# The modulation blocks that fill TensorE's gaps are issued in pairs instead of singly

## The chip, the cores and the metric

The kernel runs on one core of one Trainium2 chip. The metric is the device time of one execution in microseconds; three runs of the kernel before gave 1457.76, 1460.0 and 1465.21, so the time to beat is their median, 1460.0 us. A core has five instruction streams that run side by side and meet at semaphores: TensorE (PE, with its weight loads PEld), VectorE (DVE), ScalarE (ACT), GpSimd (POOL) and SyncE (SP), which here issues most of the transfers.

## The reference

Two layers of a hybrid block over 512 latent and 256 context tokens of width 1024. Each layer first turns the conditioning vector into six vectors per stream (adaLN), then does a mixer with three head groups (attention, a Mamba-2 scan called SSD, a Hyena long convolution) and a mixture of 16 experts:

```python
def adaln(cvec, w_mod, b_mod):                    # w_mod[i]: (1024, 6*1024)
    m = jax.nn.silu(cvec) @ w_mod + b_mod
    return jnp.split(m, 6, axis=-1)

for i in range(DEPTH):                            # DEPTH = 2
    sh1, sc1, gt1, sh2, sc2, gt2 = adaln(c, w_mod[i], b_mod[i])          # latent
    csh1, csc1, cgt1, csh2, csc2, cgt2 = adaln(c_ctx[None], w_mod[i], b_mod[i])
    hl = modulate(rmsnorm(xl, g_mix[i]), sh1, sc1)
    q_l, k_l, v_l, z_l, xbc_l, dt_l, hy_l = split_proj(hl @ w_in[i])
    ...   # attention over 768 keys; bidirectional SSD in chunks of 128; Hyena by FFT
    mix_l = jnp.concatenate([att_l, ssd_l, hyn_l], axis=-1) @ w_out[i]
    xl = xl + gt1[:, None, :] * mix_l
    hl2 = modulate(rmsnorm(xl, g_ffn[i]), sh2, sc2)
    xl = xl + gt2[:, None, :] * grouped_moe(hl2, ...)                     # top 2 of 16
    ...   # layer 0 does the same for the context tokens
return rmsnorm(xl, g_final)
```

The modulation matrix is large (6144 columns per layer, two layers) and is read for only two vectors (`c` and `c_ctx`), so its cost is mostly the transfer of its weights. Only the first two of layer 0's six vectors are needed before the first projection; all others are needed later.

## The kernel before

The 96 column blocks of the two modulation matrices (48 per layer, 128 columns each) are computed by `adaln` (L243). One block is two transfers of 256 KB into tiles called `mraw` (L254, issued on SP) and eight narrow f32 matmuls (L256), four per tile, which the trace shows as sixteen records. Four blocks share one PSUM bank (`AG = 4`); after the fourth, DVE copies the bank to `ms` (L260), and when the group after it has started its second block, `adaln_end` (L232) multiplies `ms` by a selector on PE (L238) and adds the bias on DVE (L239, tile `mcol`). The pool `md` has `MB = 4` buffers of `mraw`, which is two blocks. SP issues in order: a transfer whose buffer is still being read holds all transfers behind it.

Sixteen blocks are computed inside `norm1`, before the projections of layer 0. The other 80 are "filler": the iterator `fill` lists them, and `filler(n)` takes the next n. It is called inside the projections of layer 0 (`proj_feat`, L445, at steps k = 0, 3 and 6 of each weight block), by the generator `fillers` that is woven between the SSD, the attention heads and the attention, and in `convolutions` (two per step, `HF_ = 2`). `filler(96)` takes whatever is left before layer 0's output projection. In layer 1 the list is empty.

The order of instructions is not the written one. `weave` alternates generators by fixed ratios, and on top of that the framework reorders each engine's stream with a simulated timeline: an instruction that is ready in that timeline may be moved ahead of one that is not. So filler matmuls stand where the simulated PE would otherwise wait, and a small shift in the timeline of layer 0 can change which ready instruction comes first much later, in layer 1, where no line was edited.

Layer 1's mixer matters for the prediction. Three generators are woven after the projections: `ssd` (L720) with `attention` (L913) and `hy_conv` (L516). `ssd` goes over four chunks of 128 tokens. Each chunk needs a tile `G` of 768 KB (L731, a broadcast read issued on SP), then masks on POOL (L735), twelve exponentials on ACT (L738), a sum on POOL (L740), two products on DVE (L745), and matmuls on PE (L767 with `G`, L769 with the chunk's entering state `H`). In layer 1 `G` has one buffer (`GB = (2, 1)`), so the read for the next chunk waits until PE has read the last. `hy_conv` reads its filter tiles `Kt` (L528), also one buffer, in the same SP queue.

Of the kernel before, what the change touches and what calls it, by code (L numbers as in the profile page):

```python
# [3 lines left out]

# [136 lines left out]
def tile_kernel(tc, I, out, dbg=None):  # L141
# [89 lines left out]
    late, part = [], {}  # L231
# [10 lines left out]
    def adaln(l, ch, wp, mb, j, n, step, wp2=None):  # L242

        if j == AD:
            adaln_end()
        if j == 0:
            part["ps"] = bank("d")
        ps = part["ps"]
        for h in range(2):
            if h and wp2:  # L250
                raw = wp2.tile([P, 4, P], F32, name="mraw", tag="mraw", bufs=MB)
            else:
                raw = wp.tile([P, 4, P], F32, name="mraw", tag="mraw", bufs=mb)
            SP.dma_start(raw, I["wm"][l, :, ch, h])  # L254
            for k in range(4):
                PE.matmul(ps[32 * k:32 * k + 32, 0:P], c32[:, 4 * h + k, 30 - 2 * j:62 - 2 * j], raw[:, k],  # L256
                          start=(j + h == 0), stop=(j == n - 1 and h == 1))
        if j == n - 1:
            ms = wp.tile([P, P], F32, name="ms", bufs=2)
            DVE.tensor_copy(ms, ps[:, 0:P])  # L260
            late.append((l, slice(ch - j * step, ch + 1, step), n, ms))
# [197 lines left out]
    def proj_feat(wp, l, off, hh, hl, use, filler=None, kind="b"):  # L459
        wh, wl = wload(wp, l, off, 1024)  # L460
        for c, t0, n in ((0, 0, NLAT), (1, NLAT, NCTX)):
            if not use[c]:
                continue
            ps = bank(kind)
            for k in range(8):
                if filler and c == 0 and k in FK:
                    filler(1)
                s = slice(k * P, (k + 1) * P)
                mm3(ps[:, 0:n], wh[:, s], wl[:, s], hh[:, k, t0:t0 + n], hl[:, k, t0:t0 + n], k == 0, k == 7)
            yield c, ps[:, 0:n], n  # L470
# [7 lines left out]
    def to_tokens(src, n, cb, par, ps):  # L478
        for jt in range(n):
            PE.transpose(ps[:, jt * P:(jt + 1) * P], src[:, par + jt * 256:par + jt * 256 + 255:2], ident)  # L480

    def hy_proj(l, wp, hh, hl, pool, u, filler):

        use = (True, l == 0)
# [4 lines left out]
        for b in range(6):  # L489
            cb = b % 2  # L490
            for c, ps, m in proj_feat(wp, l, WI_HY + b * 1024, hh, hl, use, filler):
                zh, zl, x1, x2 = u[c]
                n = m // 256
                cw, cv = lv(l, VL_HW + 3 * b, 3), lv(l, VL_HB + b)
                if b >= 4:
                    conv(x2[:, cb], ps, m, cw, cv)
                    if c == len(u) - 1:
                        yield
                    continue
                d = wp.tile([P, 512], F32, name="ud", tag="ud", bufs=UB[l])  # L500
                conv(d[:, 0:m], ps, m, cw, cv)
                pt = bank("b")
                for par in range(2):
                    to_tokens(d, n, cb, par, pt[:, par * n * P:(par + 1) * n * P])
                src = pt[:, 0:2 * n * P].rearrange("p (a j w) -> p a j w", a=2, j=n)
                cs = slice(cb * P, (cb + 1) * P)
                if b < 2:
                    for par in range(2):
                        ACT.copy(zh[:, par, :, cs], src[:, par])
                        DVE.tensor_sub(zl[:, par, :, cs], src[:, par], f(zh[:, par, :, cs]))  # L510
                else:
                    for par in range(2):
                        ACT.copy(x1[:, par, :, cs], src[:, par])
                if c == len(u) - 1:
                    yield
# [1030 lines left out]
    for l in range(DEPTH):  # L1546
# [54 lines left out]
        fill = iter([(0, c) for c in range(16, 48)] + [(1, c) for c in range(48)] if l == 0 else [])  # L1601
# [6 lines left out]
            yield  # L1608

        def filler(n):  # L1610
            for _ in range(n):
                for m, c0 in fill:
                    adaln(m, c0, md, MB, c0 % AG, AG, 1)
                    break

        def fillers():
            while True:
# [136 lines left out]
        with tc.issue_after(mark.ins):  # L1754
# [5 lines left out]
            for n in (2, 4):  # L1760
                m, h = D // n, P // n
# [203 lines left out]
```

## Time and profile before

| what | value |
|---|---|
| three runs, median | 1457.76, 1460.0, 1465.21; 1460.0 us |
| the profiled execution | 1466.34 us, of which span 1464.4 us |
| PE matmul busy | 1248.4 us, 85% of the span |
| PE weight loads busy | 899.8 us, 61% |
| DVE, ACT, POOL busy | 760.8 (52%), 488.4 (33%), 453.9 (31%) us |
| mean granted TensorE clock | 0.925 |
| modulation matmuls (L256) | 1536 records, 72.8 us of PE |

PE is the busiest engine by far and its idle time is spread over all stages. A busy share is an average: what a shift in one stage is worth is read from that stage. The granted clock is shown as a share of full speed: 1.00 is 2.4 GHz and 0.50 is 1.2 GHz. Line numbers are those of the kernel before; one line is added at the top and two in `filler`, so a line below both has a number larger by three in the `order` rows of the changed kernel (by one for lines above `filler`).

### The profile page before, as it was taken

How to read it: one execution, taken by the hardware profiler on the slowest of the kernel's cores; microseconds unless marked ns; L12 is line 12 of the kernel's file. 1: busy time of each engine (PE TensorE's matmuls, PEld its weight loads, DVE VectorE, ACT ScalarE, POOL GpSimd, SP SyncE). 2: the span in 40 equal slices, each digit the busy share in tenths (PEclk: the TensorE clock that was granted, in tenths of full speed). 3: DMA queues.
4: the chain of work that ended last, by engine and by line, in shares of the span. 5: the costliest groups of instructions: out<-in, count | busy, mean ns of one | idle time of the engine just before them, and what ended most of it. 6: DMA issues, size and time to landing. Idle time of an engine off the chain costs nothing. (4 is left out here: it accounts for less than half of the span.)

```text
span 1464.4 us, 23682 instructions
## 1 busy us (share of the span) xinstructions
PE 1248.4 (85%) x8904; PEld 899.8 (61%) x8904; DVE 760.8 (52%) x1661; ACT 488.4 (33%) x1056; POOL 453.9 (31%) x497
## 2 busy tenths in 40 slices
PE   5999999899899899869998949988988888599780
PEld 2787787677677677634544428876776776345440
DVE  6854652644667875852332334754498475512121
ACT  4332334445233453311110144444454542111111
POOL 3220321544334524222323311321188412222221
PEclk9999999997799999979998969999999899699995
DMA  7744536343655163279999551111301173999954
GB/s 295 241 157 158 173 102 215 118 152 132 206 161 184 58 244 117 86 275 369 340 322 279 110 173 44 58 58 44 138 30 58 41 288 129 352 371 353 354 115 137
DMA packets 88809, 265.04 MB, mean 181 GB/s; under 512 B 10397, under 2 KB 13101, under 8 KB 88048
## 3 DMA queue, kind: packets, MB, share of 16 engines
q1 hardware_dynamic: 76016, 224.39, 43.5%
q0 software_dynamic: 12672, 39.07, 10.4%
q8 instruction: 72, 1.18, 0.3%
q14 instruction: 49, 0.40, 0.1%
HBM read 231.62 MB, written 31.79 MB: 180 GB/s over the span
## 5 line engine op out<-in xcount | busy, mean ns | idle before, releaser
L1417 PE MATMUL bank<-we,xh 128*32 128x128 f32 (+3 forms) x1280 | 208.7, 394 | 12.1 <-DVE y L1473 8.6
L1417 PEld LDWEIGHTS bank<-we,xh 128*32 128x32 f32 (+3 forms) x1280 | 99.5, 139 | 106.1 <-issue 76.9
L219 PE MATMUL bank<-hh,hw 128*128 128x512 f32 (+1 forms) x440 | 159.5, 362 | 0.1
L220 PE MATMUL bank<-hl,hw 128*128 128x512 f32 (+1 forms) x440 | 157.1, 357 | 0.0
L221 PE MATMUL bank<-hh,lw 128*128 128x512 f32 (+1 forms) x440 | 156.7, 356 | 0.4 <-DVE lw L207 0.4
L1474 POOL DMA_INDIRECT xd<-y,txi x35 | 56.6, 1618 | 177.7 <-DMA xd<-y,txi 90.2
L1417 PE MATMUL bank<-we,gh 128*32 128x256 f32 (+3 forms) x392 | 101.0, 522 | 2.8 <-ACT gh L1450 1.4
L219 PEld LDWEIGHTS bank<-hh,hw 128*128 128x128 f32 x440 | 85.4, 194 | 12.1 <-issue 1.0
L221 PEld LDWEIGHTS bank<-hh,lw 128*128 128x128 f32 x440 | 84.6, 192 | 12.8 <-DVE lw L207 0.9
L220 PEld LDWEIGHTS bank<-hl,hw 128*128 128x128 f32 x440 | 85.0, 193 | 11.4 <-issue 0.8
L930 POOL TENSOR_SCALAR pt<-pt,su 128x768 f32<-128x768 f32 (+1 forms) x60 | 55.0, 924 | 118.6 <-DVE su L929 97.6
L256 PE MATMUL bank<-mraw,c 128*32 128x128 f32 x1536 | 72.8, 295 | 16.9 <-DMA mraw<-in_wm_dram 11.8
L1393 POOL DMA_INDIRECT xg<-hd,tk x40 | 40.4, 1009 | 96.6 <-PE bank L1407 32.7
L207 DVE TENSOR_TENSOR lw<-rw,hw 128x1024 fp32r<-128x1024 f32 (+1 forms) x36 | 44.7, 1243 | 49.1 <-ACT hw L206 48.9
L256 PEld LDWEIGHTS bank<-mraw,c 128*32 128x32 f32 x1536 | 41.2, 114 | 41.4 <-DMA mraw<-in_wm_dram 16.0
L945 PE MATMUL bank<-ph,vt 128*64 128x128 f32 x624 | 53.8, 292 | 15.1 <-DVE ph L942 7.0
L1417 PEld LDWEIGHTS bank<-we,gh 128*32 128x32 f32 (+3 forms) x392 | 35.7, 143 | 49.6 <-issue 41.8
L220 PE MATMUL bank<-lo,mh 128*128 128x512 f32 x160 | 63.8, 399 | 1.5 <-DVE lo L207 1.5
L219 PE MATMUL bank<-ho,mh 128*128 128x512 f32 x160 | 64.5, 405 | 0.4 <-ACT ho L206 0.4
L221 PE MATMUL bank<-ho,ml 128*128 128x512 f32 x160 | 63.2, 395 | 0.0
L206 ACT CAST hw<-rw 128x1024 fp32r<-128x1024 f32 (+1 forms) x36 | 37.8, 1049 | 76.1 <-PE bank L220 48.0
L923 DVE TENSOR_REDUCE mx<-banks 128x1 f32<-128x768 f32 (+1 forms) x60 | 50.3, 844 | 23.3 <-PE banks L920 23.1
(478 smaller groups left out, 2744.9 us busy)
## 6 DMA issues: line engine op xcount, KB each, us to landing
we<-in_we_dram SPq DMA_DIRECT2D x192, 512.0 KB, 11.3
mraw<-in_wm_dram SPq DMA_DIRECT2D x192, 256.0 KB, 3.6
rw<-in_wi_dram SPq DMA_DIRECT2D x34, 512.0 KB, 3.5
ro<-in_wo_dram SPq DMA_DIRECT2D x16, 512.0 KB, 4.9
G<-ar SPq DMA_DIRECT2D x10, 768.0 KB, 3.9
xd<-ox SPq DMA_DIRECT2D x10, 512.0 KB, 2.7
hd<-h POOLq DMA_DIRECT2D x10, 512.0 KB, 2.9
xf<-xd SPq DMA_DIRECT2D x10, 512.0 KB, 7.0
```

The costliest lines, as they stand in the source:

```text
L206: ACT.copy(hi, src)
L207: (lo_eng or DVE).tensor_sub(lo, src, f(hi))
L219: PE.matmul(o, lh, rh, start=start, stop=False)
L220: PE.matmul(o, lh, rl, start=False, stop=False)
L221: PE.matmul(o, ll, rh, start=False, stop=stop)
L256: PE.matmul(ps[32 * k:32 * k + 32, 0:P], c32[:, 4 * h + k, 30 - 2 * j:62 - 2 * j], raw[:, k], start=(j + h == 0), stop=(j == n - 1 and h = ...
L923: DVE.tensor_reduce(mx, ps, axis=AX.XY, op=OP.max)
L930: POOL.tensor_scalar(pt[:, 0:nkt * P], pt[:, 0:nkt * P], su, 1.0, OP.mult, OP.mult)
L945: PE.matmul(po[64 * q:64 * q + 64, 0:P], vt[:, k0 + kt + j, h // 3], ph[:, (2 * j + q) * P:(2 * j + q + 1) * P], start=(kt + j == 0), stop ...
L1393: POOL.indirect_dma_start(out=xg[0:c], out_offset=None, in_=hd, in_offset=bass.IndirectOffsetOnAxis(ap=R.token(i)[0:c], axis=0))
L1417: PE.matmul(ps[r:r + c, 0:m], lh[:, 0:c], w[:, m * j:m * j + m], start=start, stop=stop)
L1474: POOL.indirect_dma_start(out=xd.rearrange("t (n m) -> (t n) m", n=n), out_offset=bass.IndirectOffsetOnAxis(ap=R.row(i)[r], axis=0), in_=y ...
```

## The change

`filler(n)` no longer issues n blocks at once. It adds n to a counter `part["due"]` and, for each two that are due, takes two blocks from the list and issues them one behind the other. In total the same 80 blocks are issued in the same sequence, and with `HF_ = 2` the calls in `convolutions` issue two at a time as before. No instruction is added or removed.

```diff
+import itertools
...
         def filler(n):
-            for _ in range(n):
-                for m, c0 in fill:
+
+            part["due"] = part.get("due", 0) + n
+            while part["due"] >= 2:
+                part["due"] -= 2
+                for m, c0 in itertools.islice(fill, 2):
                     adaln(m, c0, md, MB, c0 % AG, AG, 1)
-                    break
```

What the reordering framework makes of it differs at these places. On PE the streams are the same up to the projections of layer 0 and differ in pieces from there to the start of layer 0's attention.

Place 1, PE, layer 0, where the Hyena projections meet the first SSD steps. `mraw` is the modulation weight, `xw`/`bt`/`xb` belong to the SSD states, `ud` is a projected Hyena input, `ms` the selector product. Before:

```order
L221 MATMUL bank<-hl,hw 128x512
L256 MATMUL bank<-mraw,c_82 32x128 x8
L221 MATMUL bank<-hh,lw 128x512
L676 MATMUL bank<-cst,dm 72x128
L690 MATMUL bank<-cst,xb 128x128 x4
L256 MATMUL bank<-mraw,c_82 32x128 x8
L238 MATMUL bank<-cst,ms 128x8
L701 MATMUL bank<-xw,bt 64x192 x4
L709 MATMUL bank<-cst,xb 128x128
L690 MATMUL bank<-cst,xb 128x128 x4
L480 MATMUL bank<-cst,ud 128x128 x4
```

The same place now:

```order
L222 MATMUL bank<-hh,lw 128x512
L677 MATMUL bank<-cst,dm 72x128
L691 MATMUL bank<-cst,xb 128x128 x4
L257 MATMUL bank<-mraw,c_82 32x128 x16
L702 MATMUL bank<-xw,bt 64x192 x4
L710 MATMUL bank<-cst,xb 128x128
L691 MATMUL bank<-cst,xb 128x128 x4
L481 MATMUL bank<-cst,ud 128x128 x4
```

Two single blocks have become one pair, and the selector product has moved from right behind the block to ten matmuls of the next projection later.

Place 2, SP, the same stretch: `rw` are projection weights, `ar` and `G` the SSD's decay table and its broadcast. Before:

```order
L254 DMA mraw<-in_wm_dram 128x512 x3
L679 DMA ar_80<-act 72x128
L254 DMA mraw<-in_wm_dram 128x512
L731 DMA G<-ar_80 128x1536 x2
L254 DMA mraw<-in_wm_dram 128x512 x5
L213 DMA rw<-in_wi_dram 128x1024
L254 DMA mraw<-in_wm_dram 128x512 x7
L213 DMA rw<-in_wi_dram 128x1024
```

Now:

```order
L255 DMA mraw<-in_wm_dram 128x512
L680 DMA ar_80<-act 72x128
L255 DMA mraw<-in_wm_dram 128x512 x3
L732 DMA G<-ar_80 128x1536 x2
L255 DMA mraw<-in_wm_dram 128x512 x4
L214 DMA rw<-in_wi_dram 128x1024
L255 DMA mraw<-in_wm_dram 128x512 x8
L214 DMA rw<-in_wi_dram 128x1024
```

The transfers come in fours between two other loads, which is what the pool holds; the projection weight stands behind four `mraw` instead of five.

Place 3, SP, layer 1's mixer, where no line was edited: `Kt` is Hyena's filter tile, `G` the SSD's broadcast. Before:

```order
L528 DMA Kt<-kd1l 128x1024
L679 DMA ar_81<-act 72x128
L731 DMA G<-ar_81 128x1536
L528 DMA Kt<-kd1l 128x1024 x2
L731 DMA G<-ar_81 128x1536
L528 DMA Kt<-kd1l 128x1024
L731 DMA G<-ar_81 128x1536 x2
```

Now:

```order
L529 DMA Kt<-kd1l 128x1024
L680 DMA ar_81<-act 72x128
L732 DMA G<-ar_81 128x1536
L529 DMA Kt<-kd1l 128x1024 x3
L732 DMA G<-ar_81 128x1536 x3
```

The fourth `Kt` has moved ahead of the second `G`. On PE the same stage has changed with it: counted from the stage's first SSD matmul, 24 more of Hyena's transform matmuls (L219 to L221 on `zh`, `zl`), one more transpose (L939) and four more value matmuls (L945) stand ahead of the first chunk's state product (L769); ahead of the second chunk's stand 36 more of Hyena's inverse matmuls (on `yh`, `yl`) and three more score matmuls (L920), with four value matmuls and one transpose fewer; ahead of the third chunk's stand four more score matmuls, eight more transposes and eight more value matmuls; ahead of the fourth chunk's four more transposes and four more value matmuls.

## Rows read from the trace of the kernel before

**Rows 1.** Stages in --windows: start:end, length, each engine's busy, clock, DMA.
```profile
205.00:260.00 55.00, 51.54 (x454) 41.75 (x453) 15.43 (x27) 22.78 (x49) 8.61 (x8) 1.00 0.60 197
...
352.00:384.00 32.00, 26.95 (x192) 22.06 (x196) 13.50 (x43) 5.62 (x12) 5.27 (x9) 0.50 0.62 210
...
1046.00:1180.00 134.00, 115.26 (x884) 92.33 (x884) 99.84 (x199) 69.13 (x173) 83.65 (x85) 0.90 0.21 73
```

**Rows 2.** Timeline of PE, modulation blocks near 245 us: start, length, instruction, [idle before <-releaser].
```profile
243.40 0.64 PE L256 MATMUL bank<-mraw,c 128*32 128x128 f32 x16
244.78 0.39 PE L238 MATMUL bank<-cst,ms 128*128 128x8 f32 x2 [0.73 <-DVE ms L260]
...
254.61 0.42 PE L256 MATMUL bank<-mraw,c 128*32 128x128 f32 x8 [0.91 <-DMA mraw<-in_wm_dram]
```

**Rows 3.** Timeline of PE, modulation blocks and an SSD transpose, 312 to 352 us.
```profile
312.39 1.08 PE L256 MATMUL bank<-mraw,c 128*32 128x128 f32 x32
316.26 0.41 PE L758 MATMUL bank<-cst,ce 128*128 128x128 f32 x2 [2.79 <-DVE sy L772]
...
349.51 0.42 PE L256 MATMUL bank<-mraw,c 128*32 128x128 f32 x8 [1.09 <-DMA mraw<-in_wm_dram]
...
352.03 0.66 PE L256 MATMUL bank<-mraw,c 128*32 128x128 f32 x8 [0.63 <-DMA mraw<-in_wm_dram]
```

**Rows 4.** Clock around it: --windows, columns as in the first group.
```profile
348.00:352.00 4.00, 2.10 (x31) 1.18 (x30) 1.26 (x2) 3.85 (x12) 2.97 (x4) 0.84 0.86 280
352.00:356.00 4.00, 3.97 (x31) 3.14 (x31) 2.42 (x6) 0.95 (x3) 0.84 (x2) 0.50 0.52 171
...
384.00:388.00 4.00, 3.42 (x34) 2.33 (x27) 1.35 (x5) 3.10 (x5) 1.16 (x2) 0.89 0.70 236
```

**Rows 5.** Timeline of SP's issues, layer 1's mixer.
```profile
1055.64 0.35 SPq L731 DMA_DIRECT2D G<-ar  x1
1068.08 14.93 SPq L528 DMA_DIRECT2D Kt<-kd1l  x2
1106.89 0.32 SPq L731 DMA_DIRECT2D G<-ar  x1
1111.49 0.32 SPq L528 DMA_DIRECT2D Kt<-kd1l  x1
1130.29 19.58 SPq L731 DMA_DIRECT2D G<-ar  x2
```

**Rows 6.** Timeline of PE, layer 1's mixer: chunk products and the prices of moved groups.
```profile
1085.44 0.97 PE L920 MATMUL banks<-KT,QT 128*128 128x384 f32 x4 [0.37 <-ACT pt L927]
1086.34 0.66 PE L945 MATMUL bank<-ph,vt 128*64 128x128 f32 x8
1086.93 0.66 PE L939 MATMUL bank<-cst,pt 128*128 128x128 f32 x4
1087.34 0.38 PE L219 MATMUL bank<-yh,gh 128*128 128x256 f32 x1
...
1092.71 0.28 PE L219 MATMUL bank<-yh,gh 128*128 128x256 f32 x1
1093.07 0.28 PE L219 MATMUL bank<-yh,gh 128*128 128x256 f32 x1
...
1106.63 0.39 PE L769 MATMUL bank<-cT,H 128*64 128x128 f32 x4
...
1128.89 0.44 PE L767 MATMUL bank<-G,xtok 128*64 128x128 f32 x4
...
1145.47 0.66 PE L758 MATMUL bank<-cst,ce 128*128 128x128 f32 x4 [0.34 <-DVE G L745]
...
1148.15 0.44 PE L767 MATMUL bank<-G,xtok 128*64 128x128 f32 x4
...
1164.82 0.44 PE L767 MATMUL bank<-G,xtok 128*64 128x128 f32 x4
...
1178.68 1.09 PE L275 MATMUL bank<-cst,mcol 128*128 128x128 f32 x8 [1.81 <-DVE mixs L795]
```

## The prediction

> **What bounds the kernel now.** I first read the page's busy shares: PE is the busiest engine, so a change pays only where PE waits or where its clock falls. Then the busy time by stage [rows 1]. The filler runs in two kinds of stage. In the layer 0 projections (205 to 260 us) PE is busy 51.54 of 55 us at full clock, so there are 3.46 us of idle to win. From 352 to 384 us it is busy 26.95 of 32 us, but at half clock. The third stage that matters has no filler at all: layer 1's mixer, 1046 to 1180 us, where PE is idle 134 - 115.26 = 18.7 us at a clock of 0.90. Then the timelines, for what ends the idle time. In the projections it is the selector product waiting for DVE's copy (0.73 us) and a block waiting for its weights (0.91 us) [rows 2]. At 349 to 352 us it is the weights again (1.09 and 0.63 us) [rows 3], and right behind this gap, in which PE is busy only 2.10 of 4 us, the granted clock goes from 0.84 to 0.50 and is back near full only at 384 to 388 us (0.89) [rows 4]. In layer 1 the pace is set by a chain: `G` is read, worked on by POOL, ACT, POOL and DVE, and used by PE, and with one buffer the next read starts only when PE has read the last [rows 5, 6].
>
> **What the change adds and removes.** Nothing: the same 80 blocks, 160 transfers and 640 matmuls in the same sequence. All of the effect is order. Blocks were already issued in pairs in most places: the row at 312.39 is two blocks in one piece (32 records) [rows 3]. What is new are a few merges in layer 0 and a different interleaving in layer 1.
>
> **Layer 0, gain.** At place 1 the selector product moves behind ten projection matmuls. These are 128x256 matmuls, whose three-product step takes 0.36 us in layer 1 at full clock (1092.71 to 1093.07) [rows 6], so ten are about 1.2 us, more than the 0.73 us it waited [rows 2]: -0.7 us. If DVE's copy is late for another reason it returns at a later place, so the bound is 0. At place 2 four transfers stand before the `G` reads and the next pair reads just those four, where before a block reached for a fifth and waited 0.91 us [rows 2]: -0.9 us; bound 0, if the pair itself now waits for its fourth tile. Nothing else on PE hides behind these waits: what follows in line are projection matmuls whose weights are there. The projection weight is issued behind four filler transfers instead of five, which costs nothing, since the stage shows PE waiting on the modulation path and not on projection weights.
>
> **Layer 0, cost.** A pair needs four tiles and the pool holds four, so a fifth can't be fetched before the pair has started. In the projections other matmuls lie between pairs and cover this: from the second block of a pair at 243.40 to the block that waited at 254.61 it is 11 us [rows 2]. Without that cover, in the stretch after 337 us, a pair waits as blocks do now: 1.09 and 0.63 us [rows 3]. The demand there is the same before and after, so I expect these waits to stay. Bounds: +1.7 us if they come once more, -1.7 us if they go. I take +0.6, nearer to nothing, because the first tile of that burst is read a little later in the new order. Layer 0 in sum: -0.7 - 0.9 + 0.6 = -1.0 us.
>
> **Layer 1.** No line changed, but place 3 and the PE order did. Prices at full clock [rows 6]: three Hyena matmuls 0.36 us; four score matmuls 0.90 (1085.44 to 1086.34); four value matmuls 0.59 (to 1086.93); four transposes 0.41 (to 1087.34).
> First chunk: 24 Hyena matmuls come ahead, 24/3 x 0.36 = 2.9, plus four value matmuls 0.6 and a transpose 0.1: +3.6 us.
> Second chunk: 36/3 x 0.36 = 4.3, plus three scores 0.7, minus 0.7 for values and a transpose: +4.3 us, that is 1128.89 + 4.3 = 1133.2.
> The second `G` read stands behind the fourth `Kt`, issued at 1111.49, 4.6 us after that read's 1106.89 [rows 5]; but Hyena is ahead now, so `Kt` should be issued earlier too, and the read waits for the first chunk's products anyway. I count it inside the +3.6.
> From here the chain decides. The read follows the chunk's first product by 1.4 us (1128.89 to 1130.29), and from read to the next product it takes 22.0 us (1106.89 to 1128.89), 17.9 us (1130.29 to 1148.15) and 15.3 us (the last read, at 1130.29 + 19.58 - 0.33 = 1149.5, to 1164.82) [rows 5, 6]. The 17.9 was limited by the chain: PE waited for DVE's product on `G`, 0.34 us [rows 6]. For the third chunk: 1133.2 + 1.4 + 15.3 = 1149.9 at best, 1152.5 with 17.9. For the fourth, 15.3 + 1.4 later: 1166.6 or 1169.2, against 1164.82: +1.8 or +4.4 us. PE's own queue alone would have it only +1.0 (four transposes and four values more). I take +3. Behind it the way to the first product of the output stage (1178.68) ends in a wait on DVE `mixs`, 1.81 us [rows 6]; one attention group of 1.0 us less stands in it, half of which I credit: -0.5. Layer 1: +2.5 us.
> Bounds: if all three reads took 15.3 us, the chain is 55.2 - 45.9 = 9.3 us shorter, and with the +3.6 at its start that is -5.7; if the third chunk takes 22.0 and the fourth 17.9, it is 1133.2 + 1.4 + 22.0 + 1.4 + 17.9 = 1175.9, +11.1 us.
>
> **Sum.** -1.0 + 2.5 = +1.5 us, on the profiled execution 1466.34 to 1467.8. That execution lies 6.3 us above the median of the runs; I carry this difference over unchanged, so the same step on the median gives 1461.5 us.
>
> **A rule on the clock.** The half-clock stretch follows a gap of 1.9 us in 4 us [rows 4]. The Trainium skill, on the page TensorE: Matmul & The Clock Gate, section HAM oscillation — how this bites in real kernels, says that short bursts of matmuls with waits for transfers between them make the array fall back to its lower clock, and that the bursts then run at it. This trace agrees: 26.95 us of PE work run at 0.50 behind such a wait [rows 1]. By that rule, bursts of two blocks that find all their weights would keep the clock, and bursts that wait longer would lose it in more places; the first is the faster rival below.
>
> **Rivals.**
> 1. *The chain of `G` reads grows* (slower). As bounded above: third chunk 22.0 us, fourth 17.9, +11.1, less 1.0 from layer 0: 1470 us. For it: the read is now queued behind `Kt`, and POOL, ACT and DVE serve Hyena before the SSD. Against: most of Hyena is done by then, and the last two intervals were the short ones. It decides from a read-to-product time of about 20 us for the third chunk. Chance 0.17.
> 2. *The clock stays up behind 352 us* (faster). If the pair's tiles have landed, the gap goes and the 26.95 us of half-clock work [rows 1] shrink by 13.5 at most; the weights can't come faster, so I give it 10: with the rest of the forecast 1451.5 us. For it: the drop hangs on 1.9 us of waiting. Against: the pool has the same four buffers and the burst the same length. Chance 0.11.
> 3. *The change does not do what it says*, because the reordering had paired most blocks already, and layer 1's new order is worth the same as the old: 1460 us. For it: the many pieces of two blocks in the old order. Against: the moved chunk products. Chance 0.17.
>
> **How the numbers follow.** My forecast has 0.55 and is 1461.5 us. For three runs a side I take 0.5% (7.3 us) as what can be told from no change; the forecast and rival 3 are inside it: 0.72 same, 0.11 faster, 0.17 slower. The range takes in layer 1's low bound with layer 0's gain (1460 - 5.7 - 1.6 = 1452.7, and nearly the second rival) and the first rival: 1452 to 1471.
>
> **What would show it.** Right: one piece of 32 records at about 243 us, no wait at the selector product behind it and none of 0.9 us at 254; the half-clock stretch still at 352 to 384; in layer 1 the first chunk's state products 3 to 4 us later against the stage's start, the last 2 to 4 us later. Wrong: PE waiting for `mraw` longer in the projections than now; the clock at full at 360 us; a last chunk that comes earlier, which would mean that the chain and not PE's queue set the pace all along.

## The result: slower by about 1%, and the profile after

Six runs of the changed kernel gave 1473.77 to 1482.44 us, median 1478.92, beside 1464.26 us for six runs of the kernel before: ratio 1.0111, 95% interval 1.0082 to 1.0139. In a later session nine runs gave 1479.19 us, ratio 1.0077 [1.0047, 1.0107]. The forecast was 1461.5 us in a range of 1452 to 1471, so the direction came out and the size did not: 14.7 us slower than the six runs before, where +1.5 us was forecast. The profiled execution took 1482.44 us, of which span 1480.6; PE's busy time is 1256.5 us (+8.1), its idle time 1480.6 - 1256.5 = 224.1 us (+8.1), its mean clock 0.915 (0.925 before).

**Layer 0, place 1.** PE's modulation blocks and selector after the change, against [rows 2]:

```profile
245.18 1.08 PE L257 MATMUL bank<-mraw,c 128*32 128x128 f32 x32
...
250.65 0.28 PE L239 MATMUL bank<-cst,ms 128*128 128x8 f32 x2
...
254.48 1.08 PE L257 MATMUL bank<-mraw,c 128*32 128x128 f32 x32
```

The pair is there (32 records in one piece), and neither the selector nor the block at 254 us waits: both waits of [rows 2] are gone. But the next product, which needs DVE's `xw`, waits longer, before and then after:

```profile
245.80 0.87 PE L701 MATMUL bank<-xw,bt 128*64 128x192 f32 x8 [0.63 <-DVE xw L696]
```
```profile
247.58 0.87 PE L702 MATMUL bank<-xw,bt 128*64 128x192 f32 x8 [1.32 <-DVE xw L697]
```

These 0.69 us are nearly all of the selector's 0.73. The wait for `xw` is 1.32 us in all four traces with the new layer 0 (this one and those of e2, e9 and e12 below) and 0.63 or 0.64 in the fifteen with the old one (e15 has a third layer 0). The block's wait, 0.91 us in the trace before, lies between nothing and 0.91 us in those fifteen. From the first projection to layer 0's first state product (162.44 and 292.57 us before) it is 131.6 us in the mean of the four and 131.6 in the mean of the fifteen: by then nothing is gained.

**Layer 0, the stretch behind it.** PE's waits for weights and the selector, after the change, against [rows 3]:

```profile
351.41 0.43 PE L257 MATMUL bank<-mraw,c 128*32 128x128 f32 x8 [0.30 <-DMA mraw<-in_wm_dram]
353.09 0.43 PE L257 MATMUL bank<-mraw,c 128*32 128x128 f32 x8 [1.25 <-DMA mraw<-in_wm_dram]
354.81 0.66 PE L257 MATMUL bank<-mraw,c 128*32 128x128 f32 x8 [0.95 <-DMA mraw<-in_wm_dram]
...
377.66 0.66 PE L257 MATMUL bank<-mraw,c 128*32 128x128 f32 x8 [3.71 <-DMA mraw<-in_wm_dram]
379.58 0.65 PE L257 MATMUL bank<-mraw,c 128*32 128x128 f32 x8 [1.27 <-DMA mraw<-in_wm_dram]
...
386.19 0.39 PE L239 MATMUL bank<-cst,ms 128*128 128x8 f32 x2 [1.99 <-DVE ms L261]
```

and the later part of the same stretch before:

```profile
373.32 0.65 PE L256 MATMUL bank<-mraw,c 128*32 128x128 f32 x8 [3.74 <-DMA mraw<-in_wm_dram]
377.39 0.66 PE L256 MATMUL bank<-mraw,c 128*32 128x128 f32 x8 [0.44 <-DMA mraw<-in_wm_dram]
379.93 0.60 PE L238 MATMUL bank<-cst,ms 128*128 128x8 f32 x2 [0.84 <-DVE ms L260]
```

At 351 to 355 us the weights cost 0.30 + 1.25 + 0.95 = 2.50 us; before, it was 1.93, the 1.09 and 0.63 of [rows 3] and 0.21 at 350.15 between them. At 377 to 386 they cost 4.98 for 4.18, and a selector product behind them waits 1.99 for 0.84: +2.5 us in sum. The stretch still runs at half clock, as in [rows 4], and falls back to it once more behind the selector's wait (columns as in [rows 1]):

```profile
360.00:364.00 4.00, 4.00 (x25) 3.98 (x26) 0.00 (x0) 1.04 (x2) 0.00 (x0) 0.50 0.00 0
...
392.00:396.00 4.00, 3.56 (x12) 3.43 (x13) 1.72 (x5) 1.38 (x4) 1.82 (x2) 0.50 0.47 149
```

The Trainium skill's rule that the prediction weighed (TensorE: Matmul & The Clock Gate, HAM oscillation — how this bites in real kernels) agrees with the granted 0.50 behind the waits for weights, here as before. The faster rival built on it did not come.

Over the whole part of layer 0 that has fillers the traces agree: from the first projection to the last modulation block it is 330.1 us in the mean of the four traces with the new layer 0 (328.3 to 331.3) and 325.1 in the fifteen with the old one (321.7 to 327.4). PE idles 29.0 and 23.8 us of it, 13.9 and 10.2 right before modulation blocks and 2.9 and 1.9 right before selector products.

**Layer 1.** SP's issues after, against [rows 5], and the first state product of each of the four chunks on PE, against [rows 6]:

```profile
1067.38 0.35 SPq L732 DMA_DIRECT2D G<-ar  x1
1078.72 43.87 SPq L529 DMA_DIRECT2D Kt<-kd1l  x3
1125.05 46.76 SPq L732 DMA_DIRECT2D G<-ar  x3
```
```profile
1123.87 0.44 PE L770 MATMUL bank<-cT,H 128*64 128x128 f32 x4 [2.10 <-POOL H L719]
...
1151.96 0.39 PE L770 MATMUL bank<-cT,H 128*64 128x128 f32 x4
...
1170.36 0.39 PE L770 MATMUL bank<-cT,H 128*64 128x128 f32 x4
...
1186.30 0.48 PE L770 MATMUL bank<-cT,H 128*64 128x128 f32 x4
```

Counted from the first SSD matmul of the stage (1046.53 before, 1058.64 after), these products stand at 65.2, 93.3, 111.7 and 127.7 us; before, at 59.2, 82.6, 101.9 and 118.6 (its products at 1105.71, 1129.16, 1148.42 and 1165.08). So they are later by 6.0, 10.7, 9.8 and 9.1 us, and the first product of the output stage by 6.4. The first one waits for something new: POOL's running state `H`, 2.10 us.

PE's busy time up to the second product (columns as in [rows 1]), before and then after; the row of before that ends at the first product stands in the last section:

```profile
1105.71:1129.16 23.45, 19.86 (x162) 16.20 (x163) 21.35 (x40) 11.78 (x31) 18.53 (x18) 0.85 0.16 57
```
```profile
1058.64:1123.87 65.23, 56.16 (x420) 44.62 (x419) 54.44 (x96) 32.55 (x81) 49.33 (x45) 0.95 0.24 88
1123.87:1151.96 28.09, 23.21 (x158) 19.30 (x160) 22.38 (x42) 12.10 (x29) 18.93 (x19) 0.76 0.11 43
```

Up to the first product PE is busy 3.6 us longer (56.16 for 52.52) and idle 2.4 longer. Up to the second it is busy 7.0 us longer, the last part at a clock of 0.76 where it was 0.85, and idle 3.7 longer. The second chunk's `G` left DVE at 1144.07 us, 7.6 us before PE came to it at 1151.69, so PE's own queue set that product. For the third and fourth chunk it is 17.0 and 14.3 us from the read (1153.09 and 1171.49) to the product on `G` (1170.09 and 1185.82), and PE waits 0.29 and 0.84 us for DVE's product on `G`:

```profile
1165.75 1.54 PE L759 MATMUL bank<-cst,ce 128*128 128x128 f32 x6 [0.29 <-DVE G L746]
...
1182.62 1.16 PE L759 MATMUL bank<-cst,ce 128*128 128x128 f32 x6 [0.84 <-DVE G L746]
```

From here on one stretch serves as the measure: from layer 1's first Hyena transposes (L480) to the first matmul of its output projection, "the layer 1 stretch". Its row in the windows view (columns as in [rows 1]), before and then after:

```profile
979.52:1183.16 203.64, 180.36 (x1209) 144.75 (x1210) 127.52 (x246) 96.99 (x220) 89.11 (x91) 0.91 0.19 66
```
```profile
990.05:1203.37 213.32, 183.21 (x1210) 145.49 (x1210) 129.65 (x246) 99.08 (x222) 90.31 (x91) 0.90 0.19 69
```

It is 9.7 us longer. Length less PE's busy time is PE's idle time: 23.3 us before, 30.1 after, so 6.8 of the 9.7 us are waits; busy time times clock, the work, is 164 and 165 us. The instructions are the same.

### The profile page after: what moved, and what is told of

Same layout as the page of the kernel before. It is cut to its first block, busy times and chain, and to the rows that moved or that the text cites. A ratio compares the mean times of both kernels' runs of the same rounds, so it can differ in the third digit from the quotient of the medians.

```text
span 1480.6 us, 23687 instructions
## 1 busy us (share of the span) xinstructions
PE 1256.5 (85%) x8904; PEld 904.7 (61%) x8904; DVE 764.8 (52%) x1661; ACT 488.5 (33%) x1056; POOL 453.3 (31%) x497
## 5 line engine op out<-in xcount | busy, mean ns | idle before, releaser
L221 PE MATMUL bank<-hl,hw 128*128 128x512 f32 (+1 forms) x440 | 156.9, 356 | 0.0
L221 PEld LDWEIGHTS bank<-hl,hw 128*128 128x128 f32 x440 | 85.1, 193 | 11.5 <-issue 0.8
L221 PE MATMUL bank<-lo,mh 128*128 128x512 f32 x160 | 63.7, 399 | 1.0 <-DVE lo L208 1.0
L207 ACT CAST hw<-rw 128x1024 fp32r<-128x1024 f32 (+1 forms) x36 | 37.8, 1049 | 76.6 <-PE bank L221 43.8
L921 PE MATMUL banks<-KT,QT 128*128 128x384 f32 (+1 forms) x216 | 55.4, 378 | 8.4 <-ACT pt L928 7.6
```

Source lines behind the costliest of these rows:

```text
L207: ACT.copy(hi, src)
L221: PE.matmul(o, lh, rl, start=False, stop=False)
L921: PE.matmul(ps[:, j, 0:hw], QT[:, h, qs], KT[:, h // 3, x, ks], start=(x == 0), stop=(x == 1))
```

## The experiments

The first group holds layer 1 to a given order: a list of its 3769 instructions by engine, each bound behind the one ahead of it on its engine without any wait. Layer 1's instructions are the same in both kernels, so either order can be set behind either layer 0. The edit, the same for e1 to e8 but for the list (and e5 and e6, which have one edit more):

```diff
+        if l == 1:
+            pin(tc, nc)
         rest(0)
         close_mo()
```

**e1: layer 0 of before, layer 1 in the changed kernel's order.**

> Layer 0 as in the kernel before, word for word; in layer 1 every engine's instructions (mixer, output projection, mixture of experts) are held in the order that the changed kernel has there. Theory A (the layer 1 mixer's new order costs what its stages show: +4.3 us to chunk 0's product, +6.4 to chunk 1's, -4.3 behind it): +6 to +7 us against before, about 1470. Theory B (layer 0's merged blocks cost it, from 244 to 525 us, and layer 1's difference is the clock of that one execution): within 2 us of before, 1464. Theory C (both are noise of the clock between executions, and the 14.7 us came from a slower session): within 2 us as well.

**e2: the complement.**

> The complement: layer 0 as in the changed kernel, layer 1 held in the order of the kernel before. Theory A (layer 1 carries it): +0 to +4 us against before, 1464 to 1468. Theory B (layer 0 carries it): +8 to +12 us, 1472 to 1476. If both places add up, this run and the one above it sum to the whole difference, +14.7 us: +8 here and +6.5 there.

**e3: control.**

> Control: the kernel before with layer 1's order held to its own, so that the same instructions stand in the same places and only the holding is new. All theories: 1464 us, within 2 us of before. More than that would mean that holding the order costs something by itself, and the two runs above would have to be read against this one.

**e4: as e1, with SP's two exchanged transfers put back.**

> As the first run (layer 0 of before, layer 1 in the changed kernel's order), but SP's queue in the order of before: the second G read stands ahead of the fourth Kt again. If the place of the G read behind Kt sets the delay in layer 1, the time returns to before's, 1464 us, and the +6 of the first run is gone. If TensorE's own order (Hyena ahead of the scan) sets it, the time stays at that of the first run, within 1.5 us.

Measured against before in the same session: e1 1.0064 [1.0039, 1.0088], e2 1.0016 [0.9994, 1.0039], e3 1.0010 [0.9989, 1.0032], e4 1.0072 [1.0044, 1.0099]. The stretch in e1 and in e3:

```profile
983.37:1195.98 212.61, 181.22 (x1209) 144.07 (x1210) 130.18 (x246) 98.78 (x222) 91.11 (x91) 0.91 0.20 69
```
```profile
981.75:1185.63 203.88, 181.79 (x1210) 146.68 (x1210) 129.05 (x248) 98.43 (x221) 89.19 (x91) 0.90 0.20 69
```

Theory A stands: layer 1's order alone, in which no line was edited, makes most of the loss, and holding costs nothing that shows. PE's idle time is 31.4 us against 22.1 at the same clock, so the clock is not the cause. The `G` read behind `Kt`, to which the prediction gave room, plays no part (e4's stretch is 212.53 us, like e1's): at either place it goes out 1.3 to 1.4 us behind the first chunk's product, whose buffer it needs, as the prediction argued. Layer 0 gives +0.16%, not told from zero by the times; the stages of the traces say more: from the first projection to layer 1's Hyena transposes 822.7 us in the mean of the four with the new layer 0 (820.3 to 824.7), 816.9 in the fifteen with the old (812.9 to 821.6). That is 5.7 us, of which 5.0 lie ahead of the last modulation block; the four executions that were profiled lie 1.3 us above the medians of their kernels.

**e5, e6: relieve POOL.** In e1's trace POOL has no gap from 1098 to 1133 us. In layer 1:

```diff
-            POOL.tensor_scalar(pt[:, 0:nkt * P], pt[:, 0:nkt * P], su, 1.0, OP.mult, OP.mult)
+            ACT.activation(pt[:, 0:nkt * P], pt[:, 0:nkt * P], AF.Copy, scale=su)
```

> Layer 0 as before, layer 1 in the changed kernel's order (as the first run, 1475.4 us, +0.64% against before), but the 24 scalings of the attention's probabilities pt in layer 1 (1.1 us each in the first run's trace) stand on ACT in place of POOL. Theory A1 (the new order makes POOL the limit: it has no gap from 1098 to 1133 us in the first run's trace, and PE waits there 2.09 us for POOL's H and 3.33 us for POOL's pt): those waits go, 4 to 6 us less than the first run, 1469 to 1471. Theory A2 (PE's own queue sets it: Hyena's matmuls stand ahead of the scan, whoever made their inputs): stays within 1.5 us of the first run, 1474 to 1477. Slower than the first run if ACT, which now waits for DVE's reciprocal in its queue, becomes the limit.

> The same move of the 24 scalings to ACT with layer 1's order of the kernel before. Theory A1: POOL has little slack there too (21.1 of 24 us busy from 1082 to 1106), but PE waits only 0.4 us for pt in this order, so 0 to 3 us faster than before: 1464 to 1467 by the median of 1467.2 in the last session. Theory A2: no change. If the fifth run gains 5 us and this one nothing, POOL is what the new order overloads.

Measured: e5 1.0089 [1.0055, 1.0122], e6 0.9977 [0.9952, 1.0002]. A1 is refuted: POOL's busy time in the stretch falls from 91.11 to 63.52 us in the new order and the stretch grows to 217.46 us. PE's 2.09 us wait for `H` in e1 is gone, but the wait for `pt` comes from ACT instead (2.06 us at 1127.58), and others grow.

**e7, e8: where the loss arises.** The list is cut at the first chunk's state product: the new order up to it and the old behind (e7), and the reverse (e8).

> Layer 0 as before; layer 1 follows the changed kernel's order on every engine up to the first chunk's state product, and the order of before for all that is left then. If the loss arises ahead of that product (+2 us before the stage and +6 us in it, by the first and third runs' traces), it is +5 to +8 us against before, near the first run. If it arises behind it (+4.4 us from the first to the second product), it is +2 to +4 us.

> The complement: layer 1 follows the order of before up to the first chunk's state product, and the changed kernel's order behind it. If the loss arises ahead of that product: within 2 us of before. If it arises behind it: +3 to +5 us. If the new order's end, which is 2.8 us shorter behind the last chunk, is worth something by itself, this is the one that could come out faster than before, by up to 3 us.

Measured: e7 1.0028 [1.0002, 1.0054], e8 1.0046 [1.0024, 1.0068]. The stretch in e7 and e8:

```profile
986.32:1194.20 207.88, 180.53 (x1209) 143.82 (x1210) 127.31 (x246) 95.53 (x218) 90.39 (x91) 0.90 0.19 63
```
```profile
986.01:1197.77 211.76, 184.48 (x1209) 147.66 (x1210) 128.33 (x246) 98.43 (x222) 86.90 (x91) 0.89 0.20 69
```

PE idles 27.4 and 27.3 us: each half of the new order brings about half of the added waits, and the two ratios sum to 0.74%, about e1's 0.64. By length the halves are uneven, 4.0 and 7.9 us above e3, since PE is busy 4 us longer in e8. The loss does not sit in one place.

**e9: the change once more. e10, e11: relieve DVE**, with layer 1 held as in e1 and e3. **e12: pairs in the Hyena projections alone, no order held** (there `filler` takes the size of a group as its second argument, 1 if none is given).

```diff
-                (ACT.copy if kt % 4 else DVE.tensor_copy)(ph, ps)
+                (ACT.copy if kt % 4 or l == 1 else DVE.tensor_copy)(ph, ps)
```
```diff
-            weave((hy_proj(l, wp, hh, hl, hy0, u, filler), 1), (sg, S0[0]), stop=0)
+            weave((hy_proj(l, wp, hh, hl, hy0, u, lambda n: filler(n, 2)), 1), (sg, S0[0]), stop=0)
```

> The changed kernel as it is, beside the same runs of the kernel before as the next three. If the two parts add (layer 1's order alone +0.64%, layer 0's order alone +0.16%), it is +0.80%, 11 to 13 us, and the +1.11% of the first six runs was 4 us of luck within its interval. If it comes at +1.1% again, some 4 us belong to neither part alone.

> Layer 0 as before, layer 1 in the changed kernel's order (alone: +0.64%), but all copies ph of layer 1 on ACT, where one in three was: 24 copies of 0.69 us, 16.6 us in all, leave DVE. They wait for nothing but PE's transposes, so ACT's queue is not held by them. Theory A3 (the new order makes PE wait for results that DVE delivers late, since DVE is busy over 90% of the time up to the second chunk's product: mx 2.23 us, ph 1.95, xw 2.00, yl 1.50 in the first run's trace): half or more of the 7 us of added idle time goes, +0.0 to +0.3%. Theory A2 (PE's queue alone): +0.5 to +0.8%, as without the move.

> The same move of the copies ph with layer 1's order of before. DVE is as busy there (0.92 to 0.95 up to the second product) but PE's waits for it are short (0.4 to 1.0 us). Theory A3: 0 to 3 us faster than before, less than what the run with the new order gains. If both gain the same, DVE's load costs both orders alike and doesn't explain the difference.

> Pairs only in the Hyena projections; all other fillers single. On TensorE this gives nearly all of the changed kernel's layer 0 (all but one merged pair), but the scheduler picks a third order for layer 1: there the four chunks' state products stand at places 1154, 1242, 1342 and 1419 of PE's queue, where before they are at 1159, 1279, 1366 and 1446, and in the changed kernel at 1188, 1313, 1386 and 1454. If layer 0's pairs cost the time: +0.8% or more, as the change. If it is layer 1's order and what counts is how late the scan stands in it: no slower than before, -0.3 to +0.3% (layer 0's +0.16% included). If any order other than the one of before costs in layer 1: +0.5% or more.

Measured: e9 1.0077 [1.0047, 1.0107], about e1 and e2 added; e10 1.0072 [1.0048, 1.0097]; e11 1.0020 [0.9999, 1.0040]; e12 1.0118 [1.0080, 1.0156]. A3 is refuted as A1 was: 9.7 us less on DVE (120.53 for 130.18 us in the stretch) and no gain (214.10 us). In the old order the same move makes the stretch 4.5 us longer than e3's (208.41 us, PE idle 27.4), though the times do not show it.

e12 shows that early chunk products do not make a short stage. This third order has the chunk products early, at 56.2, 77.0, 96.2 and 112.6 us from the first SSD matmul (1057.47), which is 3.0 to 6.0 us earlier than before, and yet its ratio is the highest here and its stretch, 213.30 us with 32.6 us of idle PE, is as long as the changed kernel's. Its windows, first from the first SSD matmul to the first product, then from the second product to the end of the stretch:

```profile
1057.47:1113.66 56.19, 48.92 (x381) 39.12 (x381) 47.45 (x83) 30.27 (x74) 42.88 (x42) 0.97 0.27 100
...
1134.49:1201.62 67.13, 54.90 (x421) 44.31 (x417) 38.72 (x88) 32.80 (x78) 23.38 (x29) 0.82 0.17 59
```

What came earlier at the front is paid at the end, where attention and Hyena are left over: 67.13 us where before it took 54.00 (1129.16 to 1183.16). Behind the fourth product alone it is 31.6 us for 18.1.

**e13, e14: take vector work away instead of moving it.** In layer 1, held as in e1 and e3, the maximum reads half of the scores and the scaling covers 64 columns of a tile; the exponential's factor is 0.001 in place of 0.125 so that it stays finite (lines not shown). One execution each:

```diff
-            DVE.tensor_reduce(mx, ps, axis=AX.XY, op=OP.max)
+            DVE.tensor_reduce(mx, ps[:, 0:1] if l == 1 else ps, axis=AX.XY, op=OP.max)
...
-            POOL.tensor_scalar(pt[:, 0:nkt * P], pt[:, 0:nkt * P], su, 1.0, OP.mult, OP.mult)
+            w = 64 if l == 1 else nkt * P
+            POOL.tensor_scalar(pt[:, 0:w], pt[:, 0:w], su, 1.0, OP.mult, OP.mult)
```

> Layer 0 as before, layer 1 in the changed kernel's order, with part of the vector work of its attention left out: the scaling of pt on POOL covers 64 of 768 columns (24 times about 1 us less), the maximum on DVE reads half of the scores (24 times about 0.45 us less), and the exponential's factor is 0.001 in place of 0.125 so that it stays finite. Layer 1's attention is not computed as in the reference; only the stage from its first Hyena transposes to the first matmul of its output projection is read (212.5 us in the new order, 203.3 in the old, PE idle 31 and 23.5). Theory A4 (POOL and DVE are overloaded and the new order puts PE behind them): the stage loses more here than in the old order, and the gap of 9 us between the two falls under 4. Theory A5 (each wait comes from where an operation stands in its in-order queue, whatever the load): the gap stays at 6 us or more.

> The same work left out with layer 1's order of before. Its stage, 203.3 us, falls by 2 to 6 us; what counts is its distance to the run above: under 4 us for theory A4, 6 us or more for theory A5.

The stretch in e13 and e14:

```profile
980.00:1191.17 211.17, 181.04 (x1209) 144.56 (x1210) 124.18 (x248) 99.57 (x223) 75.06 (x91) 0.90 0.21 73
```
```profile
981.73:1177.51 195.78, 176.72 (x1210) 141.62 (x1210) 118.09 (x246) 96.67 (x219) 74.86 (x91) 0.93 0.20 70
```

Without 22 to 25 us of vector work (POOL 14 to 16, DVE 6 to 11) the old order gains 8.1 us against e3 and the new one 1.4 against e1. The gap does not close, it grows from 8.7 to 15.4 us: A4 is refuted, A5 stands. Of the 15.4 us, 11.1 are PE's idle time (9.3 between e1 and e3); the rest is its busy time, at a clock of 0.90 against 0.93. That the new order's waits hang on what stands ahead of what is the reading that is left, not shown by these two runs.

**e15: pairs in the SSD and gate projections alone** (the call of `z_proj` is changed like this one). **e16: e6 once more.**

```diff
-                yield from ssd_proj(l, wp, hh, hl, xb, filler)
+                yield from ssd_proj(l, wp, hh, hl, xb, lambda n: filler(n, 2))
```

> Pairs only in the SSD and gate projections. On TensorE layer 0 differs from before by one merged pair, and the scheduler makes a fourth order of layer 1, with 162 of 2405 PE places changed (853 in the changed kernel, 956 with pairs in the Hyena projections) and the chunk products at the same places as before. If any other order than that of before is worse, in proportion to how much is moved: +0.1 to +0.3%. If an order is a matter of chance around a middle: anywhere from -0.6 to +0.6%. If the one merged pair in layer 0 mattered, its stage from the projections to the first scan product would be 2 us longer.

> The sixth run's kernel once more (before, with layer 1's scalings of pt on ACT), which came out at -0.23% with an interval from -0.48 to +0.02. If it is really faster: -0.1 to -0.4% again, and the two sessions together exclude zero. If it was chance: within 0.15% of zero.

Measured: e15 0.9998 [0.9980, 1.0017], stretch 203.07 us; e16 0.9997 [0.9977, 1.0016]. So an order other than that of before need not cost; this fourth one leaves the chunk products and most of the rest where they were. And e6's -0.23% did not come again: no version here that does all the work beats the kernel before.

**e17, e18: single places.** In the new order two copies `ph` stand behind a subtraction `lw` on DVE. DVE around the first in e3 (old) and e1 (new), then PE's wait for it in e3 and e1 (in these kernels L961, L226 and L964 are L942, L207 and L945 of before):

```profile
1002.40 0.69 DVE L961 COPY ph<-bank 128x512 f32<-128x512 f32 x1
1003.01 0.14 DVE L943 TENSOR_SCALAR mx<-mx 128x1 f32<-128x1 f32 x1
1003.07 1.22 DVE L226 TENSOR_TENSOR lw<-rw,hw 128x1024 fp32r<-128x1024 f32 x1
```
```profile
1004.63 1.22 DVE L226 TENSOR_TENSOR lw<-rw,hw 128x1024 fp32r<-128x1024 f32 x1
1005.76 0.68 DVE L961 COPY ph<-bank 128x512 f32<-128x512 f32 x1
```
```profile
1003.15 0.66 PE L964 MATMUL bank<-ph,vt 128*64 128x128 f32 x8 [0.85 <-DVE mx L943]
```
```profile
1006.50 0.66 PE L964 MATMUL bank<-ph,vt 128*64 128x128 f32 x8 [2.23 <-DVE mx L943]
```

The value matmuls read `ph`; the profile names `mx`, the 0.14 us operation right behind the copy. They wait 1.38 us more, about the 1.22 us of `lw`. e17 puts both copies of the new order ahead of their `lw` (the second passes two more instructions), e18 puts the first of the old order behind it (it passes `mx` too):

```diff
+DVE ph<-bank
 DVE lw<-rw,hw
-DVE ph<-bank
```

> Layer 0 as before, layer 1 in the changed kernel's order but for two instructions of DVE: two copies ph (0.69 us each), which in the new order stand behind a subtraction lw (1.22 us), stand ahead of it again. Only the stage from layer 1's first Hyena transposes to its first SSD matmul is read: 68.1 to 68.9 us in five traces of the new order, 65.6 to 67.0 in the old. Theory A5 (a wait of PE comes from where one operation stands in another engine's queue): PE's two waits for these copies, 2.23 and 1.95 us, fall by about 1.2 us each, and the stage comes to 65.5 to 66.5 us; the stages behind it keep the new order's lengths (65.2 us to the first chunk's product). If PE's own order sets the stage: it stays at 68 us.

> The reverse in layer 1's order of before: the first of the two copies ph is put behind its lw, and no other instruction is moved on any engine. Theory A5: PE's wait for it, 0.85 us, becomes about 2.1, and the same stage goes from 66 to 67.2 us. If PE's order sets the stage: no change.

One execution each. PE's waits in the stage in e17, and the one in e18:

```profile
999.81 0.66 PE L964 MATMUL bank<-ph,vt 128*64 128x128 f32 x8 [1.09 <-DVE ph L961]
1002.03 0.97 PE L939 MATMUL banks<-KT,QT 128*128 128x384 f32 x4 [0.54 <-ACT pt L946]
1012.21 0.66 PE L964 MATMUL bank<-ph,vt 128*64 128x128 f32 x8 [0.78 <-DVE ph L961]
1015.52 0.74 PE L499 MATMUL bank<-cst,ud 128*128 128x128 f32 x4 [1.64 <-DVE mx L943]
```
```profile
1005.97 0.66 PE L964 MATMUL bank<-ph,vt 128*64 128x128 f32 x8 [2.48 <-DVE ph L961]
```

In e18 one exchange on DVE makes PE's wait 2.48 us instead of 0.85, and the stage's idle time 6.1 us instead of 4.5 in e3: a place in another engine's queue does make a wait of PE. The stage is 67.8 us, 2.2 longer than e3's but only 0.8 longer than before's, whose clock was lower. In e17 the two named waits fall by 1.14 and 1.17 us, as expected, but the stage stays at 68.5 us: two new waits, 0.54 and 1.64 us, stand right behind, for what DVE now does later. The expectation for the stage was missed. A reading that no run tests: PE's order in that stage asks for DVE's results closer together than DVE makes them, and an exchange on DVE alone only chooses which of them is late.

Over the whole stretch neither exchange has left a loss or a gain: e18's is 201.50 us (202.4 to 203.9 in three traces of the old order; its idle time is 26.0 us for 22.1 to 25.3, its clock 0.94), and e17's is 214.73 us (212.2 to 213.3 in four traces of the new order).

## Why the prediction was wrong

1. **The price of the moves ahead of the first two chunks is the step that failed.** They were priced as PE's matmul time at full clock and nothing else: the first chunk at +3.6 us, the second at +4.3. Measured, it was +6.0 and +10.7. Of the +6.0, 3.6 us are PE's busy time, as priced, and 2.4 are waits; of the +10.7, 7.0 are busy time, part of it at a lower clock, and 3.7 are waits. The waits are for DVE, POOL and ACT (`H` 2.1, and in e1's trace `pt` 3.3 and `yl` 1.5 us), which PE's order list cannot show. The prediction looked at the order of PE and SP in this stage, not at DVE's, ACT's and POOL's, though the trace before had DVE 95% busy between 1075 and 1099 us. With this start, layer 1's stretch came out at +9.7 us for a forecast of +2.5.
2. **"From here the chain decides" held for the third and fourth chunk and not for the stage.** Their 17.0 and 14.3 us from read to product are near the 17.9 and 15.3 of the forecast; they stand at +9.8 and +9.1 us because the second stood at +10.7. But e12 has all products early and a stretch as long, so the end of the stage does not follow from the products. What tells the old order from the new in every trace of the two is the sum of PE's waits in a stretch where attention, scan and Hyena share five queues: about 23 us in the old order (22.1 to 25.3 in three traces), 30 to 31 in the new. That is a count and not yet a cause.
3. **The stage began too late.** Some 2.0 us of the loss lie ahead of 1046 us (68.3 against 66.2 us from the Hyena transposes to the first SSD matmul, means of four and three traces), where the prediction looked at nothing.
4. **Layer 0's gain did not come.** Both named waits went, but -1.6 us was expected and nothing is left of it by the first state product. "Nothing else on PE hides behind these waits" was wrong: the wait for `xw` right behind took back 0.69 us. And the 0.91 us of the block was one trace's value, the highest of fifteen.
5. **Layer 0's cost was too small:** +0.6 with bounds of 1.7 either way. PE idles 5.2 us longer between the first projection and the last modulation block, most of it before modulation blocks: the waits that the prediction expected to stay grew. Over layer 0 the traces give +5.7 us, the times +2.4 (-0.9 to +5.7).
6. **Rival 1 had about the size (+10) but not the cause:** its third chunk was to take about 20 us from read to product and took 17.0, and e4 shows that the place behind `Kt` costs nothing. Rivals 2 and 3 did not come. That the time moved the way that was forecast is no credit either: +1.5 was a balance of -1.0, which did not come, and +2.5.

What stays open: why these orders wait as they do. The place of SP's two transfers and the clock of the stretch are out; load on POOL or DVE alone is out as far as e5, e10 and e13 lessen it. A single exchange makes a wait, as e18 shows, but none that was tried brings the stretch from one order's length to the other's, and what makes the 7 us of added waits is not shown. Whether PE's order or the vector engines' sets it was not tried.

## What to carry to other kernels

When a framework reorders instructions, an edit that adds and removes nothing can change a stage that no line touches: compare the order of all engines there. A loss is possible and not certain: of three new orders that the framework made of layer 1 here, two cost and one (e15) did not. Do not price a reordering by the busiest engine's instruction times or by one chain of milestones; count its idle time over the whole stretch. And hold the far stage's order to tell the edit's own worth from the luck of the order: here 0.16% and 0.64%.

## What was not expected of the hardware

The same stage with the same order ran at two clocks and took nearly the same time. From the first SSD matmul to the first chunk's product, before and in e2:

```profile
1046.53:1105.71 59.18, 52.52 (x386) 41.32 (x385) 47.65 (x88) 30.97 (x74) 44.32 (x44) 0.94 0.26 95
```
```profile
1055.14:1113.92 58.78, 50.02 (x387) 39.05 (x385) 48.42 (x88) 31.23 (x74) 44.26 (x44) 1.00 0.26 96
```

At 0.94 PE is busy 2.5 us longer and idle 2.1 us less, and the stage differs by 0.4 us: PE is the busiest engine there, and its busy time alone does not set the length. That DVE and POOL set it would fit e14, where less work on both shortens it to 55.9 us; which of them was not told apart.

It is no rule. e6 and e16 are one kernel, and their same stage took 57.2 us at 1.00 (1043.26 to 1100.43) and 59.2 us at 0.94 (1044.68 to 1103.90): PE was busy 50.1 and 52.8 us and idle 7.0 and 6.4. There, with POOL busy 37 to 38 us instead of 44, most of the longer busy time shows in the length. Whether a granted clock below full costs anything is read from lengths, stage by stage.
